# Program order on TensorE, and paced small steps between large products, in a two-layer hybrid encoder

## The chip, the cores and the metric

The kernel runs on one core of a Trainium2 chip. The metric is the device time of one execution in microseconds (us), lower is better; each kernel has several runs, and the median counts.

The core has a matrix engine (TensorE, PE in the profile; its weight loads are listed apart as PEld), a vector engine (VectorE, DVE), an engine for activations and copies (ScalarE, ACT), GpSimd (POOL), and SyncE (SP), whose queue issues most transfers here. Each engine works through its own list of instructions in order and waits on semaphores for the others. The kernel is written in a framework that traces the program, plans on the host in which order each engine's list stands, and sets the semaphores.

## The reference

The model is an encoder trunk of two layers over 256 tokens of width 2048, all in float32. Cut to what matters:

```python
for l in range(DEPTH):                                   # 2
    h = rms_norm(x, norm1_g[l])
    q, k, v, gu, gv = split(h @ w_in[l])                 # 1024, 256, 256, 1024, 1024
    q, k = rope(rms_norm(q, per head)), rope(rms_norm(k, per head))   # 8 query heads, 2 key heads, of 128
    attn = banded_window_attention(q, k, v, sink[l])     # |i - j| <= 128, a sink logit in the denominator
    vn = layer_norm(gelu(gv))
    f = einsum('hpq,bcqhd->bcphd', w_s, vn) + b_s        # 8 heads, within chunks of 128 tokens
    sgu = gelu(gu) * f
    mixed = concat(rms_norm(attn), rms_norm(sgu))
    x = x + mixed @ w_o[l]
    a = conv3(rms_norm(x) @ w_up[l])                     # depthwise over tokens, 2 x 5632 channels
    x = x + (silu(a_g) * a_u) @ w_down[l]
```

## The kernel before

**Precision.** A float32 product is made of three fast products: every operand is split into a `hi` part (its rounding) and a `lo` part (what is left), and hi x hi, hi x lo and lo x hi are added. Weights arrive by transfer into `raw` (three buffers), ScalarE writes `hi` (line 126, four buffers) and VectorE `lo` (line 108, four buffers); a buffer holds 1024 columns. All of this stands under `urgent()`, a priority ahead of everything that is not. Activations are split by `split_act`, `split_plain` and `parts` (lines 244 to 262), which are not urgent.

**Two ways to multiply.** `rows_by_cols` (line 146) serves the input projection of q, k, v and gv: the activations stand, 512 weight columns stream. One call is a block of four k tiles; for each k tile it issues six products of 512 columns (lines 154, 155, 157). `unit` (line 163) serves all other projections: weights stand, activations stream. For up to 16 k tiles it issues a hi run (line 187, 512 columns, as the activations' hi and lo lie side by side) and a lo run (line 197, 256 columns). The order of the two runs alternates (`after_lo`, `flipped`), so that a unit whose sum goes on in a second group of k tiles has lo products first there. `pair` (line 212) is two units of the up projection together (lines 224 and 230).

**The stages of a layer.** (1) Blocks for keys/values (`psk`) and the first four query heads (`psq`), four each, in turn. Before the last pair of blocks stand the sums of squares of the input norm (`inv_rms_cols`: a sum on VectorE at line 289, products at line 291, a scaling at line 281 and a power on GpSimd at line 283) and its broadcast to rows (`as_rows`, line 298). (2) Three more chunks of four blocks: queries of group 1, then the two halves of gv. Between their blocks the lists `steps` (lines 569 and 577) place parts of the attention: `attend` (line 369) is a generator for a group of four heads whose parts are the rotation, transposes of queries (line 387), scores (lines 265 to 268, softmax at 407 to 424), transposes of probabilities (line 436), and products with the values. `turned_keys` (line 547) transposes the keys. (3) The layer norm of gv on VectorE (lines 626 to 628), and four gate units (`gated`), between them `spatial` (line 608) and `gate`. (4) The norms of both outputs (`acca`, `accs`), and the output projection: the attention half of three units first (`pre`), then the rest. (5) The up projection with convolution and gate (`convolved`, lines 673 to 686; product at line 701), 24 channel tiles, then eight units of the down projection over them; the same for the other 20. A down unit over 24 tiles has two groups: 16 tiles (hi run 32 products, lo run 32) and 8 tiles (lo run 16, hi run 16); over 20 tiles the second group has 4 tiles (8 and 8).

**What sets the order.** The planner: it plays the program through with estimated times and takes, on each engine, the instruction of highest priority whose inputs are there; priority is the place in the program, and `urgent()` goes ahead. So TensorE's list is not the program's order. Only the first loads are kept in order (`keep_in_program_order`, line 85). Small tiles come from a pool of 42 slots (`sl`), two PSUM buffers serve all small products (`tp`), three the large ones (`mm`). `gating_tables` (line 333) loads eight tiles that the layer norm and the spatial step read; it is called at line 525, right behind stage 1.

Of the kernel before, what the change touches and what calls it, by code (L numbers as in the profile page):

```python
# [14 lines left out]
P = 128  # L15
D = 2048
# [14 lines left out]
WARM = 10  # L31
# [9 lines left out]
def encoder(ctx: ExitStack, tc: tile.TileContext, xT, w_in, w_gu, w_o, w_up, w_down, wsT, pcol, prow, rope, out):  # L41
# [41 lines left out]

    def load_first(dst, src):
        tc.keep_in_program_order(nc.sync.dma_start(dst, src))
# [5 lines left out]
    with urgent():  # L91
# [3 lines left out]
        for _ in range(WARM):  # L95
            nc.tensor.matmul(warm, ones, ones, start=True, stop=True)
# [49 lines left out]
    def rows_by_cols(ps, acts, src, first, last, raw=None):  # L146
        his, los = split_weights(src, raw)
        for kk in range(KB):
# [4 lines left out]
            for m in range(2):  # L153
                nc.tensor.matmul(ps[:, m, :], acts[kk][:, 0, ms[m]], wh, start=s0, stop=False)  # L154
                nc.tensor.matmul(ps[:, m, :], acts[kk][:, 1, ms[m]], wh, start=False, stop=False)  # L155
            for m in range(2):
                nc.tensor.matmul(ps[:, m, :], acts[kk][:, 0, ms[m]], wl, start=False, stop=s1)  # L157
# [5 lines left out]
    def unit(acts, w, ps=None, k0=0, k1=None, first=True, last=True):  # L163
# [3 lines left out]
        for g in range(k0, k1, 2 * UB):  # L167
# [15 lines left out]
            def hi_run():  # L183
                for k in ks:
                    for i in range(2):
                        x1 = acts[k].rearrange("p a b -> p (a b)")
                        nc.tensor.matmul(  # L187
                            bank[i], tile_of(his, k, i), x1,
                            start=begins and k == k0, stop=flipped and tail and k == k1 - 1,
                        )  # L190

            def lo_run():
# [3 lines left out]
                for k, i in order:  # L196
                    nc.tensor.matmul(  # L197
                        bank[i][:, :SEQ], tile_of(los, k, i), acts[k][:, 0, :],
                        start=False, stop=not flipped and tail and k == k1 - 1,
                    )  # L200

# [4 lines left out]
            else:  # L206
                hi_run()
                lo_run()
# [3 lines left out]
    def pair(acts, ws):  # L212
        pss, his, los, later = [mm(), mm()], [], [], []
        for n, w in enumerate(ws):
# [5 lines left out]
            for k in range(len(acts)):  # L220
                for i in range(2):
                    c = k % KB * UW + i * P
                    x1 = acts[k].rearrange("p a b -> p (a b)")
                    nc.tensor.matmul(pss[n][:, i, :], hs[k // KB][:, c : c + P], x1, start=k == 0, stop=False)  # L224
        for n in range(2):
            los = split_later(later) if n else los
            for k in range(len(acts)):
                for i in range(2):
                    c = k % KB * UW + i * P
                    nc.tensor.matmul(  # L230
# [34 lines left out]
    def matmul3(out, a, b, start=True, stop=True):  # L265
        nc.tensor.matmul(out, a[0], b[0], start=start, stop=False)  # L266
        nc.tensor.matmul(out, a[0], b[1], start=False, stop=False)  # L267
        nc.tensor.matmul(out, a[1], b[0], start=False, stop=stop)  # L268
# [18 lines left out]
    def inv_rms_cols(acc, n, tag):  # L287
        t = tp([P, 2])
        nc.vector.tensor_tensor(out=acc[:, 0, :], in0=acc[:, 0, :], in1=acc[:, 1, :], op=ALU.add)
        for m in range(2):  # L290
            nc.tensor.matmul(t[:, m : m + 1], acc[:, 0, m * P : (m + 1) * P], ones[:, :1], start=True, stop=True)
        return inv_rms(t, n, tag, 2)


    def as_rows(r):
        t = tp([P, SEQ])
        for m in range(2):
            nc.tensor.transpose(t[:, m * P : (m + 1) * P], r[:, m : m + 1].to_broadcast([P, P]), ident)
# [70 lines left out]
    def attend(g, ps, r, kT, v, tab, qk, nsink, acc, outs):  # L369
# [11 lines left out]
        yield  # L381
        qT = []
        for h in range(0, 4, 2):
            t = tp([P, 2, SEQ])
            for i in range(2):
                for m in range(2):
                    nc.tensor.transpose(t[:, i, m * P : (m + 1) * P], rot[m][:, h + i, :], ident)
            pq = parts(t, [P, 2, SEQ])
            qT += [[v[:, i, :] for v in pq] for i in range(2)]
        yield  # L390
        nmx = st([P, 4, 2], "nmx")
        scores = []
        for h in range(4):
# [14 lines left out]
            scores.append(s)  # L408
        sink = qk[:, R_SINK + 4 * g : R_SINK + 4 * g + 4].unsqueeze(2).to_broadcast([P, 4, 2])
# [15 lines left out]
        for pr in range(2):  # L425
            yield
# [5 lines left out]
            for b in range(2):  # L432
                t = tp([P, 2, SEQ])
                for i in range(2):
                    for m in range(2):
                        nc.tensor.transpose(  # L436
                            t[:, i, m * P : (m + 1) * P], scores[2 * pr + i][:, m, b * P : (b + 1) * P], ident
                        )
                pT.append(parts(t.rearrange("p a b -> p (a b)"), [P, W]))
            t = tp([P, W])  # L440
# [6 lines left out]
        yield  # L447
# [51 lines left out]
    for l in range(DEPTH):  # L499
# [10 lines left out]
        for b in range(NB):  # L510
            if l == 0:
                first_rows(b)
            if b == NB - 1:
# [33 lines left out]
        def turned_keys():  # L547
            t = tp([P, 2, SEQ])
            for h in range(2):
                for m in range(2):  # L550
                    nc.tensor.transpose(t[:, h, m * P : (m + 1) * P], krot[m][:, h, :], ident)
            kT.extend(parts(t, [P, 2, SEQ]))

        def chunk(c, steps):
            ps = mm()
            for b in range(NB):
                in_rows(ps, c, b)
                for step in steps[b]:
                    step()
            return ps  # L560

        def group_steps(g, ps):
            it = attend(g, ps, r1, kT, vs, tabs[0], qk, nsink, acca, att)
            return lambda: next(it)


        first = group_steps(0, psq)
        first()
# [211 lines left out]
```

## Time and profile before

| | us |
|---|---|
| median of three runs | 2024.08 (2022.14 to 2026.64) |
| the profiled execution's own time | 2021.3 |
| its span, first to last instruction | 2019.5 |
| TensorE, busy | 2009.2 |
| VectorE, busy | 1407.3 |
| ScalarE, busy | 1057.9 |

The times of instructions and windows below count from the start of the span. A group's line gives line number, engine, operation, what is written from what, and the count; behind the bar stand busy time in us, mean time of one in ns, and the idle time ahead of them. A row of the timeline is start, length, engine and operation, with the idle time ahead of it in brackets; a row of the chain is start, length and what the chain ran through. A row of the windows gives for each engine the busy us and the count, then TensorE's granted clock, the share of the transfer engines and GB/s. A matmul's time covers its way through the array, so the distance from start to start tells its cost in a stream.

### The profile page before, as it was taken

To read this page: it belongs to the slowest core of one execution; us is meant where nothing else is said; L and a number is where in the kernel's file an instruction comes from. 1 tells how busy PE (TensorE), PEld (TensorE's weight loads), DVE (VectorE), ACT (ScalarE), POOL (GpSimd) and SP (SyncE) were. 2 spreads that over 40 slices of the span, in tenths; PEclk is the share of its full clock that TensorE was granted. 3 is DMA by queue.
4 is the path that set the end of the run, shared out by engine and by line. 5 is a ranking of instruction groups with operands and counts; after the bars stand their busy time and mean duration, and the time that the engine had idled before them with its cause. 6 is when DMAs were issued, how large, how long until landed. Compare 5 with 4: busy or idle time off the path is not lost.

```text
span 2019.5 us, 28222 instructions
## 1 busy us (share of the span) xinstructions
PE 2009.2 (99%) x11324; PEld 1761.7 (87%) x11324; DVE 1407.3 (70%) x1969; ACT 1057.9 (52%) x1429; POOL 20.7 (1%) x25
## 2 busy tenths in 40 slices
PE   9999999999999999999999999999999999999999
PEld 7888888898888888888888888889888888888888
DVE  6869767777755577777667797667777555777754
ACT  6575545555533355555445655555555334555542
POOL 0000000000000000000000000000000000000000
PEclk9999999999999999999999999999999999999999
DMA  8644555455555554555565345545555554455564
GB/s 292 224 148 150 179 175 203 171 174 213 197 188 188 189 186 167 204 201 189 182 245 183 130 167 171 205 167 175 210 199 202 190 188 171 167 205 210 177 212 136
DMA packets 59891, 380.25 MB, mean 188 GB/s; under 512 B 6896, under 2 KB 9968, under 8 KB 15984
## 3 DMA queue, kind: packets, MB, share of 16 engines
q1 hardware_dynamic: 59616, 378.43, 53.6%
q8 instruction: 88, 1.44, 0.3%
q14 instruction: 43, 0.35, 0.1%
q10 hardware_dynamic: 144, 0.02, 0.0%
HBM read 376.33 MB, written 2.10 MB: 187 GB/s over the span
## 4 chain that ended last, share of the span: by engine, by line
PE 98%; DVE 1%; POOL 0%; DMA 0%; ACT 0%; SPq 0%; issue 0%; DVEq 0%
PE mm L224 30%; PE mm L187 25%; PE mm L230 16%; PE mm L197 13%; PE mm L154 3%; PE mm L157 3%; PE mm L155 3%; PE tp L187 0%; PE tp L266 0%; PE tp L608 0%; PE tp L267 0%; PE tp L268 0%; PE tp L436 0%; DMA raw<-in_w_in 0%; PE tp L197 0%; DVE sl L261 0%
## 5 line engine op out<-in xcount | busy, mean ns | idle before, releaser
L108 DVE TENSOR_TENSOR lo<-raw,hi 128x1024 fp32r<-128x1024 f32 (+1 forms) x708 | 831.4, 1214 | 414.2 <-issue 137.8
L126 ACT ACTIVATE hi<-raw 128x1024 fp32r<-128x1024 f32 (+1 forms) x708 | 731.1, 1051 | 700.0 <-PE mm L187 319.2
L224 PE MATMUL mm<-sl,hi 128*128 128x512 f32 x2688 | 617.4, 389 | 0.0
L224 PEld LDWEIGHTS mm<-sl,hi 128*128 128x128 f32 x2688 | 501.9, 188 | 102.7
L187 PE MATMUL mm<-sl,hi 128*128 128x512 f32 x2264 | 529.4, 390 | 0.0
L187 PEld LDWEIGHTS mm<-sl,hi 128*128 128x128 f32 x2264 | 419.9, 188 | 83.6
L230 PEld LDWEIGHTS mm<-sl,lo 128*128 128x128 f32 x2688 | 328.1, 192 | 3.3
L230 PE MATMUL mm<-sl,lo 128*128 128x256 f32 x2688 | 329.1, 283 | 0.0
L197 PEld LDWEIGHTS mm<-sl,lo 128*128 128x128 f32 x2264 | 282.2, 191 | 7.6 <-ACT sl L254 1.9
L197 PE MATMUL mm<-sl,lo 128*128 128x256 f32 x2264 | 287.5, 284 | 0.0
L680 DVE SCALAR_TENSOR_TENSOR sc<-ev,pc,sc 128x255 f32<-128x255 f32 x176 | 81.0, 482 | 105.5 <-ACT sc L679 105.5
L154 PE MATMUL mm<-hi,sl 128*128 128x512 f32 x320 | 126.2, 394 | 0.1
L155 PE MATMUL mm<-hi,sl 128*128 128x512 f32 x320 | 125.2, 391 | 0.0
L239 ACT COPY ev<-mm 128x512 f32<-128x512 f32 x96 | 55.6, 579 | 129.5 <-PE mm L230 114.3
L157 PE MATMUL mm<-lo,sl 128*128 128x512 f32 x320 | 99.8, 391 | 0.0
L679 ACT ACTIVATE sc<-ev,pc 128x256 f32<-128x256 f32 x176 | 98.7, 586 | 0.0
L683 DVE SCALAR_TENSOR_TENSOR sc<-ev,pc,sc 128x255 f32<-128x255 f32 x176 | 80.9, 482 | 3.0
L154 PEld LDWEIGHTS mm<-hi,sl 128*128 128x128 f32 x320 | 60.3, 188 | 12.6 <-ACT hi L126 0.6
L155 PEld LDWEIGHTS mm<-hi,sl 128*128 128x128 f32 x320 | 60.1, 188 | 11.6
L157 PEld LDWEIGHTS mm<-lo,sl 128*128 128x128 f32 x320 | 59.7, 188 | 12.0
L254 ACT ACTIVATE sl<-sl 128x256 fp32r<-128x256 f32 x88 | 32.1, 409 | 71.3 <-DVE sl L701 71.3
L241 DVE TENSOR_TENSOR ev<-mm,ev 128x512 f32<-128x512 f32 x96 | 65.6, 684 | 0.0
(124 smaller groups left out, 787.9 us busy)
## 6 DMA issues: line engine op xcount, KB each, us to landing
raw<-in_w_up SPq DMA_DIRECT2D x176, 1024.0 KB, 6.0
raw<-in_w_down SPq DMA_DIRECT2D x80, 1024.0 KB, 5.1
raw<-in_w_in SPq DMA_DIRECT2D x38, 1024.0 KB, 5.0
raw<-in_w_o SPq DMA_DIRECT2D x32, 1024.0 KB, 5.1
raw<-in_w_gu SPq DMA_DIRECT2D x16, 1024.0 KB, 5.1
raw<-in_w_down SPq DMA_DIRECT2D x16, 512.0 KB, 3.6
sl<-in_prow SPq DMA_DIRECT2D x12, 256.0 KB, 6.1
raw<-in_w_in SPq DMA_DIRECT2D x8, 256.0 KB, 5.3
```

The source lines that it names most:

```text
L108: nc.vector.tensor_tensor(out=lo, in0=part, in1=hi.bitcast(F32), op=ALU.subtract)
L126: nc.scalar.activation(hi[:, cs], part, AF.Copy)
L154: nc.tensor.matmul(ps[:, m, :], acts[kk][:, 0, ms[m]], wh, start=s0, stop=False)
L155: nc.tensor.matmul(ps[:, m, :], acts[kk][:, 1, ms[m]], wh, start=False, stop=False)
L157: nc.tensor.matmul(ps[:, m, :], acts[kk][:, 0, ms[m]], wl, start=False, stop=s1)
L187: nc.tensor.matmul(bank[i], tile_of(his, k, i), x1, start=begins and k == k0, stop=flipped and tail and k == k1 - 1,)
L197: nc.tensor.matmul(bank[i][:, :SEQ], tile_of(los, k, i), acts[k][:, 0, :], start=False, stop=not flipped and tail and k == k1 - 1,)
L224: nc.tensor.matmul(pss[n][:, i, :], hs[k // KB][:, c : c + P], x1, start=k == 0, stop=False)
L230: nc.tensor.matmul(pss[n][:, i, :SEQ], los[k // KB][:, c : c + P], acts[k][:, 0, :], start=False, stop=k == len(acts) - 1)
L679: nc.scalar.activation(t[:, i, :], s[:, i, :], AF.Identity, bias=col(3), scale=col(1))
L680: nc.vector.scalar_tensor_tensor(out=t[:, i, 1:], in0=s[:, i, : SEQ - 1], scalar=col(0), in1=t[:, i, 1:], op0=ALU.mult, op1=ALU.add)
L683: nc.vector.scalar_tensor_tensor(out=t[:, i, : SEQ - 1], in0=s[:, i, 1:], scalar=col(2), in1=t[:, i, : SEQ - 1], op0=ALU.mult, op1=ALU.add)
```

## The change

All products and transposes go through two wrappers which keep them in program order. The attention parts, the factors of the norms and the spatial step become generators that yield pauses; they are advanced by `breathe()`, called between products, against a clock `now` which only the large products advance. `gating_tables` is called behind the third chunk's products. The warm-up has nine products in place of ten. In `attend`, the pauses stand ahead of the query transposes (13.0), after each pair of them and after each of the first three scores (2.7), ahead of the transposes of probabilities (14.0 for the first, 1.4 for the others), and ahead of each product with the values (2.7). The clock is advanced after each k tile of `rows_by_cols` and within the runs of `unit`.

```diff
-WARM = 10
+WARM = 9
+    def matmul(out, a, b, **kw):
+        tc.keep_in_program_order(nc.tensor.matmul(out, a, b, **kw))
+    def transpose(out, a, b):
+        tc.keep_in_program_order(nc.tensor.transpose(out, a, b))
+    now = [0.0]
+    tasks = []
+    def task(steps):
+        tasks.append([now[0] + next(steps), steps])
+    def spend(count, cols):
+        now[0] += count * (cols / 2400 + 0.013)
+    def breathe():
+        for t in list(tasks):
+            if t[0] <= now[0]:
+                advance(t)
+    def advance(t):
+        try:
+            t[0] = now[0] + next(t[1])
+        except StopIteration:
+            tasks.remove(t)
+    def finish(n=None):
+        for t in list(tasks)[:n]:
+            while t in tasks:
+                advance(t)
...
             for m in range(2):
+                matmul(ps[:, m, :], acts[kk][:, 0, ms[m]], wl, start=False, stop=s1)
+            spend(6, W)
+            breathe()
...
+    def unit(acts, w, ps=None, k0=0, k1=None, first=True, last=True, often=False):
...
                 for k in ks:
                     for i in range(2):
...
+                    spend(2, W)
+                    if often and k % 4 == 3 and k < ks.stop - 1:
+                        breathe()
...
+                for n, (k, i) in enumerate(order):
...
+                    spend(1, SEQ)
+                    if n % 8 == 7:
+                        breathe()
...
                 hi_run()
+                breathe()
                 lo_run()
...
+    def factors(acc, n, tag, pause, got):
+        yield pause
+        r = inv_rms_cols(acc, n, tag)
+        yield 2.2
+        got += [r, as_rows(r)]
...
         nc.vector.tensor_scalar_mul(qs, qr, HD**-0.5)
-        yield
+        yield 13.0
...
             qT += [[v[:, i, :] for v in pq] for i in range(2)]
-        yield
+            yield 2.7
...
             scores.append(s)
+            if h < 3:
+                yield 2.7
...
             for b in range(2):
+                yield 1.4 if b or pr else 14.0
                 t = tp([P, 2, SEQ])
...
                 pT.append(parts(t.rearrange("p a b -> p (a b)"), [P, W]))
+            yield 2.7
             t = tp([P, W])
...
-        yield
+        if g:
+            ra = []
+            yield from factors(acc, D // 2, "a", 4.0, ra)
+            normal.extend(normed(outs, C_AG, pc, ra[1]))
...
-                r1 = inv_rms_cols(accx, D, "x")
-                r1b = as_rows(r1)
             in_rows(psk, 2, b)
+            if b == NB - 1:
+                n1 = []
+                task(factors(accx, D, "x", 0.0, n1))
             in_rows(psq, 0, b)
-        ws, lrows = gating_tables(l)
+        finish()
+        r1, r1b = n1
...
         def turned_keys():
+            yield 11.0
...
+        task(turned_keys())
+        task(attend(0, psq, r1, kT, vs, tabs[0], qk, nsink, acca, att, pc, atts))
+        ps = chunk(1)
+        task(attend(1, ps, r1, kT, vs, tabs[0], qk, nsink, acca, att, pc, atts))
...
+            ps = chunk(3 + i)
+            if i == 0:
+                ws, lrows = gating_tables(l)
...
+            s = joined(unit(acts, w_gu[l, u], often=True))
...
-        ra = inv_rms_cols(acca, D // 2, "a")
+        def spatials():
+            for u in range(4):
+                yield 3.0 if u else 2.0
+                spatial(u)
+                if u < 2:
+                    gate(u)
         gated(0)
-        atts = normed(att, C_AG, pc, as_rows(ra))
         gated(1)
-        for u in range(2):
-            spatial(u)
-            gate(u)
+        task(spatials())
         gated(2)
-        for u in range(2, 4):
-            spatial(u)
+        gated(3)
+        finish()
         gate(2)
-        gated(3)
         gate(3)
...
+        task(factors(accs, D // 2, "s", 6.0, rs))
+        pre = [unit(atts, w_o[l, u], None, 0, NK // 2, last=False, often=True) for u in range(3)]
+        finish()
         with urgent():
-            rs = as_rows(inv_rms_cols(accs, D // 2, "s"))
-            mixT = atts + normed(sg, C_SG, pc, rs)
-        pre = [unit(atts, w_o[l, u], None, 0, NK // 2, last=False) for u in range(3)]
+            mixT = atts + normed(sg, C_SG, pc, rs[1])
...
                 if f == 0:
+                    n2 = []
+                    task(factors(accx, D, "y", 6.0, n2))
                     ps = unit(acts2, w_up[l, f // 2])
-                    r2 = inv_rms_cols(accx, D, "y")
                     ps2 = unit(acts2, w_up[l, NF // 2])
-                    r2b2.append(as_rows(r2).unsqueeze(1).to_broadcast([P, 2, SEQ]))
+                    finish()
+                    r2b2.append(n2[1].unsqueeze(1).to_broadcast([P, 2, SEQ]))
```

More of the change, by code (lines that the diff above doesn't have):

```diff
@@ L95, in encoder @@
         for _ in range(WARM):
-            nc.tensor.matmul(warm, ones, ones, start=True, stop=True)
+            matmul(warm, ones, ones, start=True, stop=True)
         first_raws = [rawp.tile([P, 4 * W], F32, tag="raw", name="raw") for _ in range(2)]
@@ L290, in inv_rms_cols @@
         for m in range(2):
-            nc.tensor.matmul(t[:, m : m + 1], acc[:, 0, m * P : (m + 1) * P], ones[:, :1], start=True, stop=True)
+            matmul(t[:, m : m + 1], acc[:, 0, m * P : (m + 1) * P], ones[:, :1], start=True, stop=True)
         return inv_rms(t, n, tag, 2)
+    def factors(acc, n, tag, pause, got):
[3 more added lines that the diff above has]
+        got += [r, as_rows(r)]
     def as_rows(r):
@@ L557, in chunk @@
                 in_rows(ps, c, b)
-                for step in steps[b]:
-                    step()
-            return ps
[L562 to L568, printed above, removed]
-        ps = chunk(1, [[], [], [turned_keys], [first]])
-        second = group_steps(1, ps)
-        second()
+            return ps
+        atts = []
+        task(turned_keys())
+        task(attend(0, psq, r1, kT, vs, tabs[0], qk, nsink, acca, att, pc, atts))
+        ps = chunk(1)
+        task(attend(1, ps, r1, kT, vs, tabs[0], qk, nsink, acca, att, pc, atts))
         vn = []
@@ L607, in spatial @@
                 for m in range(2):
[L608 removed]
+                    matmul(
                         f[:, h, m * P : (m + 1) * P],
```

38 lines of the change are left out of this document (16 added, 22 removed).

## The prediction

> **What bounds the kernel now.** I read the page first, then the chain of work that ended last, then TensorE's products by line and shape, then its waits, and last the timeline where its order differs from the program's.
>
> ```profile
> span 2019.5 us, 28222 instructions
> PE 2009.2 (99%) x11324; PEld 1761.7 (87%) x11324; DVE 1407.3 (70%) x1969; ACT 1057.9 (52%) x1429; POOL 20.7 (1%) x25
> ```
>
> TensorE is busy for 99% of the span and is the bound. The reader is to see how little is left: an order of issue can win only what TensorE spends beyond streaming. The chain gives the cadence of an undisturbed run.
>
> ```profile
> 322.90 14.53 PE mm L224 x64
> 337.43 7.67 PE mm L230 x64
> 1174.78 1.79 PE tp L608 x16
> 2014.63 0.96 PE tp L197 x8
> ```
>
> So a product of 512 columns takes 14.53/64 = 0.227 us, one of 256 takes 0.120, one of 128 takes 0.11. The counts, and the first large product:
>
> ```profile
> L224 PE MATMUL mm<-sl,hi 128*128 128x512 f32 x2688 | 617.4, 389 | 0.0
> L187 PE MATMUL mm<-sl,hi 128*128 128x512 f32 x2264 | 529.4, 390 | 0.0
> L230 PE MATMUL mm<-sl,lo 128*128 128x256 f32 x2688 | 329.1, 283 | 0.0
> L197 PE MATMUL mm<-sl,lo 128*128 128x256 f32 x2264 | 287.5, 284 | 0.0
> L154 PE MATMUL mm<-hi,sl 128*128 128x512 f32 x320 | 126.2, 394 | 0.1
> L187 PE MATMUL tp<-sl,hi 128*128 128x512 f32 x40 | 9.4, 390 | 0.0
> L266 PE MATMUL tp<-sl 128*128 128x256 f32 x32 | 9.3, 290 | 0.0
> L266 PE MATMUL tp<-sl 128*128 128x512 f32 x16 | 6.9, 433 | 0.6 <-DVE sl L261 0.6
> 5.34 0.56 PE L154 MATMUL mm<-hi,sl 128*128 128x512 f32 x1
> ```
>
> Lines 155 and 157 have the count of 154, lines 267 and 268 that of 266, and the last unit has 40 products at 197 beside its 40 at 187. That is 4992 + 960 + 48 = 6000 products of 512 columns (1362 us), 4992 + 96 = 5088 of 256 (610 us), and what is left of 11324 without the 20 of the warm-up, 216 small ones, at 0.11 (24 us): 1996 us. From 5.34 to 2015.59 TensorE had 2010.2 us. **About 14 us is all that better pacing can return**, some 0.7%.
>
> ```profile
> PE tp L298 <- POOL xr L283: 2.1, 2, 1.6
> PE tp L551 <- DVE sl L540: 1.0, 1, 1.0
> ```
>
> The named waits are the largest pieces: the broadcast of the norm factor waits for the power on GpSimd, and the turned keys wait for VectorE. The rest is a few tenths at each attention or norm product.
>
> **The change, part by part.** Every product and transpose now goes out in the order in which the code makes it. Before, the planner was free to swap them; a stalled TensorE cannot swap. I look for places where it had swapped to good purpose. There are four, all alike: the first unit of each half of the down projection, in both layers. Lines 203 to 205 put the second run of that unit as all lo products, then all hi ones. The newest activations (the last pair of `ys`) come at its end.
>
> ```profile
> 552.08 5.43 PE L197 MATMUL mm<-sl,lo 128*128 128x256 f32 x44
> 553.23 4.63 DVE L108 TENSOR_TENSOR lo<-raw,hi 128x1024 fp32r<-128x1024 f32 x4
> 557.78 0.48 DVE L680 SCALAR_TENSOR_TENSOR sc<-ev,pc,sc 128x255 f32<-128x255 f32 x1
> 558.81 0.69 DVE L701 TENSOR_TENSOR sl<-sl,sc 128x512 f32<-128x512 f32 x1
> 560.36 0.70 ACT L254 ACTIVATE sl<-sl 128x256 fp32r<-128x256 f32 x2
> 560.81 0.81 PE L197 MATMUL mm<-sl,lo 128*128 128x256 f32 x4
> 907.65 4.47 PE L197 MATMUL mm<-sl,lo 128*128 128x256 f32 x36
> 908.80 4.63 DVE L108 TENSOR_TENSOR lo<-raw,hi 128x1024 fp32r<-128x1024 f32 x4 [1.77 <-PE mm L197]
> 911.96 4.27 PE L187 MATMUL mm<-sl,hi 128*128 128x512 f32 x18
> 915.77 0.42 ACT L254 ACTIVATE sl<-sl 128x256 fp32r<-128x256 f32 x1 [0.71 <-DVE sl L701]
> 916.24 0.51 PE L197 MATMUL mm<-sl,lo 128*128 128x256 f32 x2
> ```
>
> In the first half 44 lo products run, 32 of the first run and 12 of the second's 16; the last 4, on the newest tiles, come only at 560.81, with hi products drawn ahead in between. In program order they are due at 552.24 + 44 x 0.120 = 557.5. The tiles are not there: VectorE made four weight splits (urgent ones, 4.63 us) before it took up the last convolution at 557.78, its gating product ended at 559.50, and the activation split of 0.35 to 0.4 us follows, at best to 559.9. **TensorE waits 2.4 us** (bounds 2.4 and 3.2, up to when it resumed here). In the second half 36 lo products are done at 912.1, and the next need the split that began at 915.77 and let them go at 916.24: **4.1 us**. The hi products that covered this (18 of them at 911.96) stand behind the wait now, and so do all later products; VectorE's splits ahead of the convolution are freed by the lo run itself, so they come just as before. Two halves, two layers: 2 x (2.4 + 4.1) = **13 us added**. The bounds are 0, should the convolution be put before those splits, and 2 x (3.2 + 4.1) = 15.
>
> The paced steps. A block of the input projection has four quarters of six products. Each quarter advances the clock `now` by 6 x (512/2400 + 0.013) = 1.358 us, and a task goes out at the first end of a quarter after its pause. Its own products are not counted in `now`. Three things are then late.
>
> (a) The input norm. Its two steps, which stood almost side by side and cost waits of at most 1.6 us, stand 2 quarters apart now, 2.7 us, so that wait goes. But the sums go out after the first quarter of the last query block, 4.1 us before that ends, and the factor some 1.6 us behind them, so the scaled copies of keys and queries start later, 2.5 us before the end. In the second layer:
>
> ```profile
> 1056.44 0.45 PE mm L157 x2
> 1052.01 1.25 ACT L533 ACTIVATE sl<-mm,xr 128x512 f32<-128x512 f32 x2
> 1068.61 0.69 DVE L360 TENSOR_TENSOR sl<-sl 128x512 f32<-128x512 f32 x1
> 1172.98 0.35 PE tp L291 x4
> ```
>
> The block ends at 1056.89, the keys were copied 4.9 us before, and the last query rotation ended at 1069.30, 12.4 us behind it. Copied 2.4 us later, it ends 14.8 us behind; TensorE's transposes come after ten quarters, 13.6 us, and four turned keys, at 14.0. I take 1 us of wait a layer (bounds 0 and 3).
>
> (b) VectorE's load. With pauses of 13, 14, 2.7 and 1.4 us, by my count of quarters the last attention product goes out at `now` = 78.1 and the sums for its norm at 83.5, counted from the block's end. With some 17 us of the steps' own products that is 100.5 us, where it was 1172.98 - 1056.89 = 116.1.
>
> ```profile
> 1052.00:1176.00 124.00, 123.13 (x634) 103.21 (x633) 96.98 (x166) 77.14 (x125) 8.01 (x5) 1.00 0.46 153
> ```
>
> VectorE has 97 us of work in that stretch of 124, and would have it in about 108: 90% busy in place of 78%. Splits of attention tiles are not urgent and queue behind weight splits of 1.2 us and, after the last value block, behind the layer norm of the gating rows (twelve passes, 8 us at the 0.69 of line 701), which the code now makes before the last attention steps. TensorE stands still for each that is late. I take 3 us a layer; the bounds are 0, as there is still slack, and 15.6, where nothing of the pull forward is had.
>
> (c) The second output norm. Its sums go out 7.35 us behind the last gate unit (pause 6, first chance after it).
>
> ```profile
> 187.18 0.59 ACT L239 COPY ev<-mm 128x512 f32<-128x512 f32 x1 [1.08 <-PE mm L197]
> 195.60 0.61 ACT L600 ACTIVATE sl<-ev 128x512 f32<-128x512 f32 x1
> 200.33 0.41 DVE L289 TENSOR_TENSOR sl<-sl 128x256 f32<-128x256 f32 x1
> ```
>
> The chain from copy to sums ended at 200.74, 13.6 us behind the unit. The steps by themselves are these three, 1.6 us, and five passes at some 0.69, 5.1 in all; with half a split (0.6 us) ahead of each of the five on VectorE, and half a microsecond ahead of the three on ScalarE, 9.5. I take 2 us a layer (bounds 0, and 13.6 - 7.35 = 6.3).
>
> So of the 14 us that are returned, 2 x (1 + 3 + 2) = 12 come back as new waits (bounds 0 and 2 x (3 + 15.6 + 6.3) = 50).
>
> The gating tables move from before the keys to behind the first value block: eight loads, which pass the weight loads on SP's queue.
>
> ```profile
> sl<-in_prow SPq DMA_DIRECT2D x12, 256.0 KB, 6.1
> ```
>
> Cost nothing: they are first used after the second value block, over 21 us later, and weights that are loaded two blocks ahead hide them; without that cover, one landing, 6.1 us a layer. They free eight of 42 slots for attention meanwhile. The sums for the FFN norm move up to the end of the first unit's hi run:
>
> ```profile
> 277.80 7.28 PE mm L187 x32
> 284.30 0.42 DVE L289 TENSOR_TENSOR acc<-acc 128x256 f32<-128x256 f32 x1
> ```
>
> That run ends at 285.08 and VectorE had its part ready at 284.72: nothing, or a few tenths. One warm-up product less is nothing: TensorE goes on to wait for a weight load at 9.95 us either way (at most 0.4 us).
>
> **The sum:** -14 + 12 + 13 = +11 us; I round to +10, as each wait also lets VectorE catch up. On the profiled execution's 2021.3 us (span 2019.5 and 1.8 around it) that is 2031; the median of the three runs, 2024.08, stands 2.8 above it, which gives **2034 us**.
>
> [...] No pause of TensorE in this trace is over 1.6 us once it runs, and its granted clock is 1.00 throughout. In the warm-up its products went at half pace:
>
> ```profile
> 1.05 4.34 PEld L96 LDWEIGHTS tp<-ones 128*128 128x128 f32 x20 [1.05 <-DVE ones L92]
> ```
>
> That is 0.217 us for 128 columns, against 0.11 later. If a wait of 4.1 us puts the clock back for as long as the warm-up, each costs another 4.34/2 = 2.2 us; twice, that makes 2034 + 4 = 2038. [...]
>
> **The rivals.**
> 1. Forecast: waits at the down projection and late attention tiles outweigh what is returned, +2 to +18 us. Chance 0.45.
> 2. The clock falls in the long waits: 2038. [...] 0.05.
> 3. VectorE falls well behind in attention (12 a layer, 24 in all, not 6): -14 + 30 + 13 = +29, 2053; from +18 on I count it here. For it the 90%; against it that waits relieve it. 0.12.
> 4. Faster: the last convolution is put ahead of the four weight splits of line 108. From two of the four on this decides: 2 x 1.16 us earlier, the tiles of the first half come at 557.6 for 557.5; all four earlier, those of the second at 911.6 for 912.1. The 13 us is gone, and with waits of 7 us, not 12, it is -14 + 7 = -7: 2017. For it that the order on VectorE is planned anew; against it that those splits are urgent and the convolution is not. 0.28.
> 5. The change leaves the order at the down projection as it is, or gains and waits cancel: 2024. 0.10.
>
> **Chances.** A measurement of this kernel tells 0.2% (4 us) from no change. Of the first, 0.07 lies within 4 us; of the fourth, 0.22 beyond. Faster 0.22, same 0.07 + 0.06 + 0.10 = 0.23, slower 0.38 + 0.05 + 0.12 = 0.55. The range leaves out most of the third above, and the lowest end of the fourth: 2014 to 2046. The forecast's own range is 2026 to 2042.
>
> **What would show it.** Right: TensorE's waits name ACT line 254's tile at the four first down units, 2.4 and 4.1 us each, with 48 and 40 lo products unbroken; the wait for the power is gone; waits for splits (line 261) and for the sums of `accs`. Wrong: those units run through, or VectorE's convolution stands before the splits; then the fourth rival holds. Over 6 us of attention waits in a layer means the third.

## The result: slower by 3.4%, and the profile after

The changed kernel takes 2093.56 us (median of four runs, 2091.52 to 2095.40) against 2023.94 for the kernel before (four runs): a ratio of 1.0343, interval 1.0325 to 1.0360. The sign was forecast, the size was not: 2093.56 lies far above the range of 2014 to 2046. The profiled execution took 2093.65 us. From its page: the span, the engines, and the granted clock by slices.

```profile
span 2091.8 us, 28223 instructions
PE 2030.7 (97%) x11322; PEld 1778.2 (85%) x11322; DVE 1410.7 (67%) x1969; ACT 1059.9 (51%) x1429; POOL 19.2 (1%) x25
PEclk9989999999999999999999899999999999999999
```

VectorE and ScalarE have the work they had (1410.7 for 1407.3, 1059.9 for 1057.9). TensorE is busy 21.5 us longer with the same products, and two slices, the third and the 23rd, show a lower clock: the attention stage of each layer. The span grew by 72.3 us. TensorE's waits, by what ended them (total, times, longest); line 306 writes the lo part of an attention tile, 305 its hi part, 299 the hi part of an activation for a projection, 478 is the softmax's reciprocal, 334 the sum ahead of a norm, 676 the sum behind the spatial products, 412 the rotation:

```profile
PE tp L85 <- DVE sl L306: 26.1, 9, 7.4
PE mm L85 <- ACT sl L299: 15.2, 5, 5.4
PE tp L85 <- ACT sl L305: 6.7, 4, 2.3
PE tp L85 <- DVE rec L478: 3.1, 1, 3.1
PE tp L85 <- DVE sl L334: 2.0, 2, 1.0
PE tp L85 <- DVE sl L676: 1.9, 2, 1.0
PE tp L88 <- DVE sl L412: 1.1, 1, 1.1
```

These are 56.1 us; of such tiles the list of before has only 0.6, for the lo part of attention tiles. All waits that the list of before names, but for the one at the warm-up, are 5.1 us. For the rest I took each product's distance to the next one's start and subtracted the prediction's cadences (0.227, 0.120, 0.11; a record of 512 columns itself lasts 0.389). The excess over the whole trace is 16.8 us before and 89.3 after, and the difference, 72.5, is the growth of the span (72.3). Of the 89.3, the waits above are 56.1, products streamed at half clock cost 20.0 more than their cadence, and 13.2 is what is left beside them. (Of the 16.8 before, 11.7 is left beside the named waits: that remainder didn't shrink.) **So pacing returned 16.8 - 13.2 = 3.6 us, and the new order costs 56 us of waits and 20 us of clock.**

The longest wait, in the timeline of the changed kernel:

```profile
147.78 0.57 ACT L305 ACTIVATE sl<-tp 128x512 fp32r<-128x512 f32 x1
...
148.91 1.00 DVE L683 TENSOR_SCALAR vn<-vn,mv,lnr 128x512 f32<-128x512 f32 x2 [0.81 <-POOL lnr L648]
149.83 1.29 DVE L684 TENSOR_TENSOR vn<-vn,sl 128x512 f32<-128x512 f32 x2
...
154.36 1.29 DVE L685 TENSOR_TENSOR vn<-vn,sl 128x512 f32<-128x512 f32 x2
155.56 0.68 DVE L306 TENSOR_TENSOR sl<-tp,sl 128x512 fp32r<-128x512 f32 x1
156.30 1.22 PE L85 MATMUL tp<-sl 128*128 128x512 f32 x2 [7.40 <-DVE sl L306]
```

All twelve passes of the layer norm, 6.7 us, stand on VectorE ahead of one split of 0.68 us for which TensorE stands still. The hi part of that tile, the first row, was ready at 148.35, while VectorE stood idle: it kept to its list and waited until 148.91 for the factor (line 648) of the first pass. The same place in the second layer (1197.62) costs 7.39. On ScalarE it is the softmax:

```profile
118.66 1.28 ACT L472 ACT_TABLE_LOAD   x1
119.95 0.51 ACT L472 ACTIVATE sl<-sl,nm 128x256 f32<-128x256 f32 x1
...
124.85 0.19 ACT L475 ACTIVATE es<-es 128x8 f32<-128x8 f32 x1
124.95 0.57 ACT L305 ACTIVATE sl<-tp 128x512 fp32r<-128x512 f32 x1
125.58 0.49 PE L85 MATMUL tp<-sl 128*128 128x512 f32 x1 [2.33 <-ACT sl L305]
```

Eight exponentials with their reads, a table load of 1.28 us ahead of them and one weight split among them hold the list for 6.2 us; the tile that TensorE needs for the other group of heads comes behind them. And at the second half of the down projection:

```profile
936.22 4.84 DVE L144 TENSOR_TENSOR lo<-raw,hi 128x1024 fp32r<-128x1024 f32 x4 [1.66 <-PE mm L85]
940.99 0.87 DVE L741 SCALAR_TENSOR_TENSOR sc<-ev,pc,sc 128x255 f32<-128x255 f32 x2
...
942.68 0.69 DVE L764 TENSOR_TENSOR sl<-sl,sc 128x512 f32<-128x512 f32 x1
943.41 0.72 ACT L299 ACTIVATE sl<-sl 128x256 fp32r<-128x256 f32 x2 [3.60 <-DVE sl L764]
943.88 1.22 PE L85 MATMUL mm<-sl,lo 128*128 128x256 f32 x4 [4.34 <-ACT sl L299]
```

Here the forecast mechanism stands as it was described: four weight splits, then the convolution, its product, the split, and TensorE waiting. The four places cost 2.50, 4.34, 2.78 and 5.41 us.

Is VectorE full in the attention stage? The same 85 us in both kernels (columns: TensorE, weight loads, VectorE, ScalarE, GpSimd, clock, share of the transfer engines, GB/s), first after:

```profile
95.00:180.00 85.00, 67.79 (x314) 54.94 (x313) 49.20 (x85) 44.49 (x74) 1.39 (x2) 0.88 0.38 124
```

and before:

```profile
95.00:180.00 85.00, 84.72 (x458) 71.56 (x457) 66.76 (x117) 56.16 (x99) 1.39 (x2) 1.00 0.44 143
```

It isn't: 49.2 of 85 us. Every engine does less there, as all wait for TensorE, which waits for one instruction at a time. A low share under these waits doesn't yet show that load isn't the cause; run 6 below does, where VectorE is busier and TensorE waits less.

### The profile page after: what moved, and what is told of

The parts are those of the page before. It is cut to its first block, busy times and chain, and to the rows that moved or that the text cites. A ratio compares the mean times of both kernels' runs of the same rounds, so it can differ in the third digit from the quotient of the medians.

```text
span 2091.8 us, 28223 instructions
## 1 busy us (share of the span) xinstructions
PE 2030.7 (97%) x11322; PEld 1778.2 (85%) x11322; DVE 1410.7 (67%) x1969; ACT 1059.9 (51%) x1429; POOL 19.2 (1%) x25
## 4 chain that ended last, share of the span: by engine, by line
PE 90%; DVE 6%; ACT 3%; issue 1%; DMA 0%; POOL 0%; DVEq 0%; ACTq 0%; SPq 0%
PE mm L85 88%; DVE lo L144 3%; PE tp L85 2%; ACT hi L162 1%; ACT sl L472 1%; PE tp L88 0%; DMA raw<-in_w_down 0%; DVE sl L306 0%; DVE sc L514 0%; DVE sl L300 0%; ACT sl L299 0%; DVE ev L286 0%; DVE ev L655 0%; DVE sl L483 0%; ACT vn L639 0%
## 5 line engine op out<-in xcount | busy, mean ns | idle before, releaser
L85 PEld LDWEIGHTS mm<-sl,hi 128*128 128x128 f32 x4952 | 931.2, 190 | 190.4 <-ACT hi L162 0.2
L85 PE MATMUL mm<-hi,sl 128*128 128x512 f32 x640 | 179.4, 403 | 0.0
L85 PE MATMUL tp<-sl 128*128 128x256 f32 (+1 forms) x144 | 32.4, 351 | 35.9 <-DVE sl L306 26.1
L554 DVE TENSOR_TENSOR xs<-mm,xs 128x512 f32<-128x512 f32 x80 | 54.8, 685 | 11.5 <-PE mm L85 11.3
L736 DVE TENSOR_TENSOR ev<-ev,rb 128x512 f32<-128x512 f32 x88 | 60.1, 683 | 0.1
L85 PEld LDWEIGHTS tp<-sl 128*128 128x128 f32 x144 | 23.1, 199 | 43.5 <-DVE sl L306 24.0
L300 DVE TENSOR_TENSOR sl<-sl 128x256 fp32r<-128x256 f32 x88 | 33.5, 422 | 22.0 <-ACT sl L299 22.0
L292 DVE SCALAR_TENSOR_TENSOR sl<-xs,pc,sl 128x256 fp32r<-128x256 f32 x64 | 29.8, 482 | 14.8 <-ACT sl L291 14.8
```

The source lines that it names most:

```text
L85: tc.keep_in_program_order(nc.tensor.matmul(out, a, b, **kw))
L300: nc.vector.tensor_tensor(out=t[:, 1, :], in0=src, in1=t[:, 0, :].bitcast(F32), op=ALU.subtract)
L554: nc.vector.tensor_tensor(out=xs[u], in0=ps[:, :, a : a + SEQ], in1=xs[u], op=ALU.add)
L736: nc.vector.tensor_tensor(out=s, in0=s, in1=r2b2[0], op=ALU.mult)
```

## The experiments

Theory A, formed from this trace: TensorE in program order stands for every tile that is late, and tiles are late because work of less need stands ahead of them on VectorE and ScalarE; the pauses are a side matter. Rival B: the pauses put the steps at the wrong times, and the order of the lists matters little. For the clock: the half-clock windows are a cost of their own, or they only lie where TensorE waits anyway. The kernel before took 2022.3 to 2023.9 us on the chips of these runs. A run with no interval is a single execution; executions of the kernel before lie up to 5.3 us apart on one chip (2020.98 to 2026.30), those of the changed one 3.9, so 2 or 3 us between single ones show nothing by themselves.

**1. Program order alone.** The kernel before with only the two wrappers.

```diff
+    def matmul(out, a, b, **kw):
+        tc.keep_in_program_order(nc.tensor.matmul(out, a, b, **kw))
...
-                nc.tensor.matmul(ps[:, m, :], acts[kk][:, 0, ms[m]], wh, start=s0, stop=False)
+                matmul(ps[:, m, :], acts[kk][:, 0, ms[m]], wh, start=s0, stop=False)
```

> The kernel before with its products and transposes kept in program order, and nothing else changed. Theory A (a TensorE that cannot swap waits wherever an input is late, and then runs at half clock for some windows): the four first down units cost as in the changed kernel (waits of 2.5 to 5.6 us, 23 us with the half clock), and attention without pauses waits more than with them: 2080 us or more, waits for line 261's splits far above 26 us. Theory B (it is the new placing of the steps that costs, and the order alone is cheap apart from the down units): 2024 + 23 = 2047 us, with the down units' waits and few others.

Measured: 2151.71, +129 us. Its longest waits (line 295 is the sum ahead of a norm, 436 the scaling of the probabilities, 260 the hi part of an activation for a projection, 405 the score masking):

```profile
PE tp L85 <- DVE sl L295: 30.8, 4, 8.4
PE tp L88 <- DVE sl L436: 15.8, 4, 5.2
PE mm L85 <- ACT sl L260: 14.8, 4, 5.4
PE tp L85 <- DVE sl L405: 12.4, 6, 5.1
```

The order is the cost, and the tasks with their pauses take back 58 us of it (2151.7 to 2093.6). They do nothing for the third row, the down projection, which the tasks don't touch. One sign of theory A didn't come: the waits for the splits (line 261 of the kernel before, 267 here) are 10.1 us, not far above 26. Without pauses TensorE waits at the steps ahead of the splits.

**2. Tasks alone.** The changed kernel, with the planner free on TensorE.

```diff
-        tc.keep_in_program_order(nc.tensor.matmul(out, a, b, **kw))
+        nc.tensor.matmul(out, a, b, **kw)
```

> The changed kernel with its products and transposes free to be swapped again; tasks, pauses and the later tables stay. Theory A: the planner swaps around late tiles, no wait over 2 us, the clock stays full, 2018 to 2030 us. Theory B: the layer norm still stands ahead of the attention splits on VectorE and the steps are early, so long waits stay: over 2045 us.

Measured: 2034.12, between the two bounds: +12 against the kernel before on that chip, -59 against the changed one. Theory A's "no wait over 2 us" and full clock didn't come true: two waits are 2.5 and 2.6 us, and the clock is at half for 6.83 us from 1213.72. The new places of the steps in the program are a loss of some 12 us even where the planner may swap; B has that much, A the other 59.

**3. The down projection free.** Only its products leave the program order.

```diff
-                unit(ys, w_down[l, u, :, f0 * UW : f1 * UW], ps)
+                unit(ys, w_down[l, u, :, f0 * UW : f1 * UW], ps, mul=nc.tensor.matmul)
```

> The changed kernel with only the products of the down projection free to be swapped. Theory A: the four waits for line 299's tile (2.5, 4.3, 2.8 and 5.4 us) and the half clock behind them go, 22 to 23 us less than the changed kernel: 2070 to 2072 us, with 48 and 40 lo products broken up again. Rival (the wait is only put off to the next unit, as VectorE is late there anyhow): less than 10 us off, over 2083 us.

Measured: 2072.52, -21.0. Of the four waits, 15.0 us, one of 1.4 stays; the other 7 us are clock, as products at half clock cost 12.1 here and 20.0 in the changed kernel.

**4. The layer norm's code behind the second gate unit.** The six lines of 679 to 685 move down.

```diff
-        for i in range(2):
-            for m in range(2):
-                t = vn[2 * i + m]
...
         gated(0)
         gated(1)
+        for i in range(2):
+            for m in range(2):
+                t = vn[2 * i + m]
...
```

> The changed kernel with the twelve passes of the gating rows' layer norm made behind the second gate unit in place of ahead of the first. Theory A (the split of the transposed probabilities stands behind these passes in VectorE's list): the two waits of 7.4 us go, with one or two half-clock windows at each (1.7 us a window): 18 to 22 us less than the changed kernel, 2071 to 2076 us. Rival (VectorE is full there, whatever stands first): the wait moves to the spatial step, less than 8 us off, over 2085 us.

Measured: 2080.75, -12.8; less than the 18 to 22 expected, more than the rival's 8. The 7.4 us became 1.2, with the split now after one pass:

```profile
149.44 0.55 DVE L697 TENSOR_SCALAR vn<-vn,mv,lnr 128x512 f32<-128x512 f32 x1 [0.81 <-POOL lnr L648]
149.90 0.68 DVE L306 TENSOR_TENSOR sl<-tp,sl 128x512 fp32r<-128x512 f32 x1
```

Two waits shorter by 6.2 are 12.4 us; the half-clock windows there shrank from 10.24 to 3.41 us, but most of that was idle time, so the clock returned only about 2 us. New waits for hi parts of weights (line 162) took 1.6 back. I had counted the clock fuller.

**5. The waits of the down projection filled.** Ten (first half) or eighteen (second half) products on ones, ahead of the four that wait; the trace has two passes for each, 20 and 36. The wait itself isn't shortened, only TensorE kept busy in it.

```diff
+                    if fill and flipped and tail and n == len(order) - 4:
+                        spare = tp([P, P])
+                        for _ in range(fill):
+                            matmul(spare, ones, ones, start=True, stop=True)
```

> The changed kernel with spare products of ones (10 calls, some 2.2 us, in a first half and 18, some 4.0 us, in a second) ahead of the four products that wait in the first down units; nothing reads them. Theory A (the half clock of 3.4 or 6.8 us at these four places comes from TensorE standing still): the clock stays full there, what is left of the wait stays, and the four places cost some 16 us in place of 23: 6 to 8 us less than the changed kernel, 2086 to 2088 us. Rival (the clock falls for another reason, as at the start of a heavy stretch): the half clock stays and nothing is won, 2093 us or more.

Measured: 2087.25, -6.3. The windows of the same 7 us, first of this kernel, then of the changed one:

```profile
942.00:949.00 7.00, 6.90 (x35) 5.74 (x34) 4.13 (x8) 3.95 (x7) 0.00 (x0) 1.00 0.18 62
```

```profile
942.00:949.00 7.00, 5.12 (x14) 4.25 (x15) 2.56 (x6) 1.18 (x3) 0.00 (x0) 0.51 0.28 115
```

None of its half-clock stretches lies at the four places. The clock is a cost of its own: 6.3 / 4 = 1.6 us a place.

**6. Attention's splits urgent.** The two instructions of `parts` get the priority of weight splits.

```diff
+        with urgent():
             nc.scalar.activation(hi, src, AF.Copy)
             nc.vector.tensor_tensor(out=lo, in0=src, in1=hi.bitcast(F32), op=ALU.subtract)
```

> The changed kernel with the splits of attention tiles (parts) made urgent, as the weight splits are. Theory A (the waits in attention come from the order in ScalarE's and VectorE's lists, where a run of exponentials or the layer norm stands ahead of the split): of 36 us of waits in attention some 8 are left, and most half-clock windows there go: 35 to 50 us less, 2043 to 2058 us. Theory B (VectorE is too full for the paced steps, 90% busy): the waits turn up at other inputs or at weight splits, under 20 us less, over 2073 us.

Measured: 2057.66, -35.9 us, for a priority: no instruction was taken out, no pause changed. The waits for lines 305 and 306 fell from 32.8 us to one row of 2.6 (307 here). This is the run that settles the main cause for A. In the 85 us of the comparison above VectorE now does more work than in the changed kernel, 62.45 for 49.20 us, or 73%, and TensorE is still busier, so the load was not what held the splits up:

```profile
95.00:180.00 85.00, 79.36 (x425) 67.70 (x424) 62.45 (x112) 54.26 (x97) 1.86 (x2) 0.98 0.47 157
```

Theory B has a small share: the sum ahead of a norm (335 here, 2.0 us in the changed kernel), the scaling of the probabilities (484, no row before) and the rotation (413, 1.1 before) now cost more than they did. Of the attention, norm and spatial waits, 40.9 us in the changed kernel, run 6 has 17.8. All but the spatial sum's 1.9:

```profile
PE tp L85 <- DVE sl L335: 6.9, 4, 2.5
PE tp L88 <- DVE sl L484: 3.9, 2, 2.0
PE tp L85 <- DVE sl L307: 2.6, 2, 1.3
PE tp L88 <- DVE sl L413: 2.5, 1, 2.5
```

**7. Runs 3 and 6 together.**

> The changed kernel with both: urgent splits of attention tiles, and the down projection's products free to be swapped. Theory A: the two gains add up (-35 to -50 and -21): 2022 to 2037 us, few half-clock windows. Theory B: over 2052 us.

Measured: 2046.16, -47.4 where -56.9 is the sum of the two: between both expectations. The missing 9.5 us is clock. Products at half clock cost 20.0 us in the changed kernel, 12.1 in run 3 and 8.9 in run 6 beyond their cadence; the two reductions together would leave 1.0, but 10.4 are there. The waits in the attention stages are nearly the same in both runs, but run 6 has one half-clock stretch there and this run has five: the same 1.9 us wait cost one here and none in run 6 (last section). That it is luck how such a wait meets the clock's grid is my reading; it isn't shown.

**8. Late gating tables and nine warm-up products,** in the kernel before (ten executions).

```diff
-WARM = 10
+WARM = 9
-        ws, lrows = gating_tables(l)
...
+            if i == 0:
+                ws, lrows = gating_tables(l)
```

> The kernel before with the two minor edits alone: nine warm-up products, and the gating tables loaded behind the third chunk. Both theories: within 0.2% of before (2020 to 2028 us). If the later loads or the shorter warm-up had a share in the loss it would show here as more.

Measured: 2021.28, ratio 0.9988, interval 0.9978 to 0.9997: nothing, or a hair faster, as forecast for both edits. The wait of 1.0 us for the turned keys (line 551 of the kernel before) is gone from its list.

**9. Longer pauses,** on run 7: 16, 17, 4.0, 7, 8 and 4 in place of 13, 14, 2.7, 4, 6 and 2 (four executions).

```diff
-        yield 13.0
+        yield 16.0
-                yield 1.4 if b or pr else 14.0
+                yield 1.4 if b or pr else 17.0
...
```

> The kernel of e7 (urgent splits of attention tiles, down projection free) with longer pauses: 16 and 17 in place of 13 and 14 ahead of query and probability transposes, 4.0 in place of 2.7 ahead of the product with the values, 7 in place of 4 and 8 in place of 6 ahead of the norm sums, 4 in place of 2 ahead of the first spatial step. Theory A (the paced steps only come before their inputs are ready): the 20 us of waits in e7 fall under 6, no half clock in the two attention stages, 2016 to 2026 us, as fast as before or faster. Theory B (some wait follows the steps wherever they stand): over 2035 us.

Measured: 2046.03, ratio 1.0108 (1.0094 to 1.0121): not a microsecond gained, the rival's outcome. The waits of run 7 left, and others came:

```profile
PE tp L85 <- DVE sl L452: 10.5, 4, 2.8
PE tp L85 <- DVE sl L677: 5.6, 2, 2.8
PE tp L88 <- ACT sl L500: 2.5, 2, 1.2
```

Score masking (452) had no row in run 7; 677 is the spatial sum, 500 the copy of the product with the values. At the masking it is the list again: the scores of one head were done at 108.11, but on VectorE two weight splits and two passes of the statistics of gv (line 641) stand ahead, with an idle stretch of 1.50 us for a hi part of weights, so the masking starts at 113.13 and TensorE goes on at 114.14, 2.81 us late. With longer pauses other steps come to stand behind work of less need; for rows 677 and 500 that isn't shown.

**10. Two broadcasts later,** in the kernel of run 8 with TensorE's order free (nine executions).

```diff
-                r1b = as_rows(r1)
             in_rows(psk, 2, b)
+            if b == NB - 1:
+                r1b = as_rows(r1)
...
-        atts = normed(att, C_AG, pc, as_rows(ra))
         gated(1)
+        atts = normed(att, C_AG, pc, as_rows(ra))
```

> The kernel of e8 (free order, tables late, nine warm-up products) with the broadcast of the input norm put behind the last key block, and that of the attention norm behind the second gate unit. What the changed kernel meant to win, without its order: the waits for the power of 2.1 and 0.5 us go, 2 to 4 us less than e8: 2017 to 2020 us, ratio to before 0.997 to 0.9985. Rival (the planner finds other waits): 2021 us or more.

Measured: 2018.88, ratio 0.9975, interval 0.9965 to 0.9985: **faster than both kernels.** It takes 5.0 us less than the kernel before on that chip; run 8 was measured on another. The wait for the input norm's power (2.1 us before) is gone. That for the attention norm's, which the second move was to remove, is still 0.5, and one wait is new, 0.9 for the hi part of an activation (line 254):

```profile
PE mm L197 <- ACT sl L254: 0.9, 1, 0.9
PE tp L298 <- POOL sr L283: 0.9, 2, 0.5
PE tp L298 <- POOL ar L283: 0.5, 1, 0.5
```

**11. Run 7 with the late layer norm of run 4,** and **12. the same with all of attention's steps urgent** (four executions):

```diff
+        with urgent():
             nc.vector.tensor_tensor(out=acc[:, 0, :], in0=acc[:, 0, :], in1=acc[:, 1, :], op=ALU.add)
...
+            with urgent():
+                nc.scalar.copy(o.rearrange("p a b -> p (a b)"), t)
+                add_squares(acc, o, g == 0 and pr == 0)
```

> Kernel: urgent tile splits in attention and a free order in the down projection, as in the run of 2046, and in addition the layer norm's twelve passes written behind the second gate unit. In that run of 2046 TensorE waited 2.5 us in each layer (near 164 and 1177) for the sum of the attention norm, which stood on VectorE behind six of those passes, and a half-clock window of 6.83 us followed each. Theory (list order: each wait is caused by work of lower need that stands ahead on VectorE): both waits and both windows go, 2 x (2.5 + about 2) = 9 us, 2035 to 2039. Rival (the paced steps are too tight for the chain whatever stands ahead): the waits stay or turn up at the spatial step, over 2043.

> Kernel: the one before, and in addition every step of attention on VectorE and ScalarE (rotation, score masking, softmax, scaling of the probabilities, copies and squares, sum for the norms) under urgent priority, so that weight splits queue behind them and not the other way. Theory (list order alone): the waits left, 3.9 for the scaled probabilities, 2.5 for the rotation, 2.3 for late splits, go as well; 2022 to 2032, near the kernel before. Rival (weight splits pushed back make the large products wait instead): waits for the hi or lo weight tiles appear, over 2040.

Measured: 2037.05 and 2042.73 (ratio 1.0090, 1.0073 to 1.0106). The first is as theory A had it: -9.1 us against run 7, the two waits at 164 and 1177 shrank from 2.5 to 1.1, and the half-clock windows behind them went. The second is a miss for A alone, and the rival's outcome: 5.7 us slower than the first. TensorE waits longer for the lo parts of attention tiles (2.3 before), and now a weight split comes too late for the large products:

```profile
PE tp L85 <- DVE sl L307: 5.8, 4, 2.0
...
PE mm L85 <- DVE lo L144: 2.0, 1, 2.0
```

So A explains what can be had by changing one rank, down to about 2037. **What stays open** is the last 14 us to the kernel before (run 11 still has 17.3 us of waits, where before has 5.1): no set of pauses and priorities that I tried brought program order to par, and I can't say whether one exists. Run 2 shows that about as much (12 us) is lost with the planner free, so part of it may lie in the steps' new places; that it is the same 12 us is not shown.

## Why the prediction was wrong, point by point

**The bound** was right: TensorE, with little to return. But the first term of the sum, -14, was mis-sized: I put the whole ceiling into it. By start-to-start distances, 3.6 of 16.8 came back. The waits that the list of before names, mostly for the power and the keys, are 5.1 us; the remainder beside them was 11.7 before and is 13.2 after, so nothing of it came back. So most of the 14 us were, as far as these traces tell, no waits that this pacing could remove.

**The down projection** was right: 13 us forecast for 2.4 and 4.1 us in two layers, 15.0 measured, with VectorE's four splits ahead of the convolution as the row of before showed. The fourth rival, the convolution put first, didn't come about.

**(a) and (c)** were right in kind: 1 us a layer for the rotation, measured 1.1 in the first and none in the second; 2 us a layer for the second output norm, measured 1.0 in each. Not priced: 1.0 a layer at the spatial step.

**(b) is the step that failed.** "I take 3 us a layer": the waits for lines 305, 306 and 478 are 26.1 + 6.7 + 3.1 = 35.9 us, 18 a layer. That lies above even the upper bound of 15.6. The reason was wrong as well. I reckoned with VectorE's load, 90%, and read its 10% of slack as a buffer. The load in that stretch is 58%, and run 6, with 73%, waits less; it was the rank that counted. A non-urgent instruction ranks by its place in the program, and the pacing moved the last attention steps behind the code of the layer norm. I named those twelve passes, "8 us at the 0.69 of line 701", and then let them vanish in an average. As TensorE may not swap, they had to be read as one wait: 7.4 us. In the kernel before, the planner set splits (line 261) between the passes (626 to 628), as its timeline of VectorE shows:

```profile
153.99 1.00 DVE L626 TENSOR_SCALAR vn<-vn,mv,lnr 128x512 f32<-128x512 f32 x2 [0.81 <-POOL lnr L591]
154.91 0.69 DVE L627 TENSOR_TENSOR vn<-vn,sl 128x512 f32<-128x512 f32 x1
155.51 0.68 DVE L261 TENSOR_TENSOR sl<-tp,sl 128x512 fp32r<-128x512 f32 x1
```

**The third rival** had the right sign, more than 6 us a layer in attention (18.5 with the rotation, over 20 with the norms and the spatial step), and a chance of 0.12. Its mechanism, VectorE falling behind by its load, was not the one that came; its 2053 was too low for the same reason as (b) and for the clock.

**The second rival**, the clock, had 0.05 and two places. Its price was right: 2.2 us each, against 20.0 / 11 = 1.8. The count was wrong. That only the two waits of 4.1 us would lower the clock was my estimate, and no run shows it: the trace has eleven stretches at half clock, and one begins at 126.34 behind a wait of 2.33 us (up to 125.58), another at 170.72 behind one of 2.34 (up to 170.56).

The sum of +11 becomes the +72 between the profiled executions (the medians are 69.6 apart) by these terms: attention, norm and spatial waits 41 for 12, down projection 15 for 13, clock 20 for none, returned 3.6 for 14; that is 29 + 2 + 20 + 10 = 61 us.

**The edits costed at nothing** (tables, warm-up, FFN norm) cost nothing: run 8, and no row for the FFN norm's sums in the waits of after.

## What to carry to other kernels

Before fixing an engine's order, read in the other engines' lists what stands directly ahead of each instruction that the fixed engine will wait for; a burst of low-need work there was the wait here, at its full length (7.40 us behind passes of 6.7), at a mean load of 58%. Then give the small producers the rank of what depends on them: here the priority of two instructions was worth 36 us, longer pauses nothing. Where order is left free, move single steps by a block (run 10): with the edits of run 8 that returned 5 us of the 14, and one wait of 0.9 us came in its place.

## What the runs showed of the hardware

In the trace of the changed kernel TensorE's clock changes on a fixed grid. All eleven half-clock stretches are 3.41, 6.83 or 10.24 us long, and their starts lie whole multiples of 3.413 us apart, from 126.34 to 1983.20. Windows of that grid, in the changed kernel (first number after the length: TensorE's busy us; the clock is the first figure behind the five engines):

```profile
122.93:126.34 3.41, 0.82 (x3) 0.19 (x1) 1.52 (x7) 2.60 (x11) 0.00 (x0) 1.00 0.61 173
126.34:129.75 3.41, 2.44 (x6) 1.96 (x7) 1.97 (x7) 1.14 (x2) 0.00 (x0) 0.50 0.33 137
109.28:112.69 3.41, 2.11 (x10) 1.46 (x9) 3.11 (x6) 0.19 (x1) 0.00 (x0) 1.00 0.92 266
```

A window busy for 0.82 of 3.41 us, 24%, is followed by one at half clock; one busy for 62% is not. Of the changed kernel's full-clock windows (behind the first 20 us) the eleven that were busy for 39% or less were each followed by half clock, and none of the others, which were all busy for 62% or more. Between these figures the runs show both: run 4's window from 1195.31, busy for 1.48 us (43%), kept the clock, and one wait of 1.87 us, for the scaled probabilities, went both ways. In run 7:

```profile
102.55:105.96 3.41, 1.54 (x8) 0.87 (x6) 3.41 (x10) 0.05 (x1) 0.00 (x0) 1.00 0.75 308
105.96:109.37 3.41, 3.41 (x10) 2.71 (x11) 1.86 (x6) 1.56 (x2) 0.00 (x0) 0.50 0.02 5
```

and in run 6, where TensorE was busy a little longer in the window:

```profile
100.16:103.57 3.41, 1.60 (x8) 0.99 (x7) 3.16 (x8) 0.64 (x2) 0.00 (x0) 1.00 0.86 345
103.57:106.98 3.41, 3.35 (x18) 2.76 (x19) 2.64 (x9) 1.90 (x3) 0.00 (x0) 1.00 0.03 5
```

So of the idle time within one window, 1.87 us (run 7: 3.41 - 1.54) and 2.59 us (the changed kernel: 3.41 - 0.82) were followed by half clock, and 1.81 us (run 6: 3.41 - 1.60) was not. Run 4 kept the clock behind 1.93 us, so the idle time of one window alone doesn't tell it in these runs.
